# The attention softmax's maxima and sums: two row layouts swapped through DRAM instead of by matmuls on tables

## The chip, the cores and the metric

The kernel runs on one core of a Trainium2 chip. The metric is device time in microseconds (us). The core's engines run side by side and wait for each other through semaphores: TensorE (PE; its weight loads are listed apart as PEld), VectorE (DVE), ScalarE (ACT), GpSimd (POOL) and SyncE (SP). SP and POOL issue the DMAs that matter here; all of them share sixteen DMA engines.

## The reference

One layer of a decoder trunk on a sequence of 512 tokens with 1024 features: a feed-forward half step, a mixer of an attention branch and an mLSTM branch, and a second feed-forward half step. The change touches the attention branch alone: four head slots, and in each slot three groups with (window, dilation) = (128, 1), (512, 4), (2048, 16). The outputs of a slot's groups are added with weights that come from each group's maximum m and sum l:

```python
    m = jnp.max(s, axis=-1)
    p = jnp.exp(s - m[..., None])
    l = jnp.sum(p, axis=-1)
    ...
    lse = jnp.moveaxis(m + jnp.log(l), -1, 2)
    ...
    alpha = jax.nn.softmax(jnp.stack(lses, axis=0), axis=0)
    att = jnp.sum(alpha[..., None] * jnp.stack(outs, axis=0), axis=0)
```

So for each token the maxima and sums of the groups must meet.

## The kernel before

The projections are float32 products, each split into three passes of a reduced-precision matmul: every weight tile of 128x1024 is loaded by SP (`wf`, three buffers), cast on ACT to a high half (`wh`) and subtracted on DVE to a low half (`wl`, both with five buffers, line 99), and PE multiplies high by high, high by low and low by high (`ws`, line 189: 24 matmuls of 512 columns for each of two tiles of a group).

The attention part handles one head slot h after another. `scores(h)` computes the score blocks in PSUM, and DVE adds the mask and takes each row's maximum. The tile `val` holds, for 128 partitions, the maxima in `val[:, 0, :]` and the sums in `val[:, 1, :]`. Its columns 0 to 3 belong to the first group, whose rows lie in blocks of 128 tokens in a row (token = 128*b + p: the "natural" layout). Its columns 4 to 7 belong to the two dilated groups, masked and reduced together, whose rows lie by residue class (token = 4*p + j: the "class" layout). ACT then computes the exponentials (line 929), whose row sums are the second half of `val`.

`exchange(h)` brings both layouts together. DVE multiplies the values with 0/1 tables (`perm`, loaded once by POOL) into two spread tiles, `ln` and `lc` (lines 937 and 939, 128x128 each, for maxima and for sums). PE then multiplies these with two more tables into a PSUM bank `pe` (lines 943 and 945; a float32 matmul of the program counts as two in the trace). From `pe` DVE reads the other layout's maxima `om` and sums `ol`: `mm` (joint maximum), `ee` (two differences, exponentiated on ACT, line 954), `l` (two products), `w` (sum, reciprocal, product), and last the scaling of the eight score blocks `sm` by `w` (line 964). `turn(h)` transposes the scaled blocks on PE into the banks `pt` (line 973) and ACT copies them to `pT`; `values(h)` multiplies them with the attention values.

Program order puts other work between these: for h = 1, 2, 3 the loop runs `qk_proj(h, 0)`, `exchange(h - 1)`, `qk_proj(h, 1)`, `turn(h - 1)`, `qk_proj(h, 2)`, `values(h - 1)` and `scores(h)`. The last slot's `exchange(3)` stands between two projections of the mLSTM branch (tile `pm`, followed on DVE by a convolution whose steps write `z`), and `turn(3)` stands in the middle of the second of them. A list scheduler merges the code into one instruction order for each engine; each engine then runs its list strictly in order.

POOL's list is short in this part: constants, then for each pair of slots a store of the projected values to a DRAM scratch tensor (`v12rows`, line 897) and a load of it in class layout (`v`, line 899).

Of the kernel before, what the change touches and what calls it, by code (L numbers as in the profile page):

```python
# [10 lines left out]
F32 = mybir.dt.float32  # L11
# [3 lines left out]
ALU = mybir.AluOpType  # L15

P = 128
T = 512
# [21 lines left out]
def tile_hybrid_block(ctx: ExitStack, tc: tile.TileContext, a: dict):  # L40
    nc = tc.nc
# [20 lines left out]
    def bank(name):  # L62
        return psum.tile([P, 512], F32, tag="pp", name=name)

    def pair(name):
        return [bank(f"{name}_{b}") for b in range(2)]
# [65 lines left out]
    dram = ctx.enter_context(tc.tile_pool(name="dram", bufs=1, space=bass.MemoryType.DRAM))  # L132
# [667 lines left out]
    ap_ = actx.enter_context(tc.tile_pool(name="attn", bufs=1))  # L800
# [5 lines left out]
    masks = ap_.tile([P, 512], BF16, name="masks")  # L806
    with tc.issue_after(mixer_from):
        nc.gpsimd.dma_start(masks, a["masks"])
    perm = ap_.tile([P, 72], F32, name="perm")
    nc.gpsimd.dma_start(perm, a["perm"])  # L810
    by4, by32, mod4, div32 = perm[:, 0:32], perm[:, 32:64], perm[:, 64:68], perm[:, 68:72]
    gb = mix.tile([4, 2], F32, name="gb")
    with tc.issue_after(mixer_from):
        nc.gpsimd.dma_start(gb, a["gbias"])
# [89 lines left out]
    def scores(h):  # L904
        q = [qk_of[h, g] for g in range(3)]
        ps0, ps1 = pair(f"ps0{h}"), pair(f"ps1{h}")
        for tb in range(NT):
            lo = 0 if tb else P
            nc.tensor.matmul(ps0[tb // 2][:, tb % 2 * 256 + lo:(tb % 2 + 1) * 256], lhsT=q[0][:, 0, tb * P:(tb + 1) * P],
                             rhs=q[0][:, 1, max(tb - 1, 0) * P:(tb + 1) * P], start=True, stop=True)  # L910
        for g in (1, 2):
            for j in range(NT):
                o = j % 2 * 256 + (g - 1) * P
                nc.tensor.matmul(ps1[j // 2][:, o:o + P], lhsT=q[g][:, 0, j * P:(j + 1) * P], rhs=q[g][:, 1, j * P:(j + 1) * P], start=True, stop=True)
        sm = ap_.tile([P, 8, 256], F32, tag="sm", bufs=1, name=f"sm{h}")
        val = small.tile([P, 2, 8], F32, tag="val", name=f"val{h}")
        nm = small.tile([P, 8], F32, tag="nm", name=f"nm{h}")
        for half, ps in enumerate((ps0, ps1)):
            for i in range(NT):
                lo = P if half == 0 and i == 0 else 0  # L920
                nc.vector.tensor_tensor_reduce(out=sm[:, 4 * half + i, lo:], in0=ps[i // 2][:, i % 2 * 256 + lo:(i % 2 + 1) * 256],
                                               in1=masks[:, half * 256 + lo:(half + 1) * 256], scale=1.0, scalar=NEG,
                                               op0=ALU.add, op1=ALU.max,
                                               accum_out=val[:, 0, 4 * half + i:4 * half + i + 1])
            hs = slice(4 * half, 4 * half + 4)
            nc.vector.tensor_scalar(nm[:, hs], val[:, 0, hs], -SC, None, op0=ALU.mult)
        for i in range(8):
            lo = P if i == 0 else 0
            nc.scalar.activation(sm[:, i, lo:], sm[:, i, lo:], AF.Exp, scale=SC, bias=nm[:, i:i + 1],
                                 accum_out=val[:, 1, i:i + 1])  # L930
        return sm, val

    def exchange(h, sm, val):
        ln = ap_.tile([P, 8, 32], F32, tag="ln", bufs=1, name=f"ln{h}")
        lc = ap_.tile([P, 2, 32, 4], F32, tag="lc", bufs=1, name=f"lc{h}")
        for v in range(2):
            nc.vector.tensor_tensor(ln[:, 4 * v:4 * v + 4, :], val[:, v, 0:4, None].broadcast_to([P, 4, 32]),
                                    by4[:, None, :].broadcast_to([P, 4, 32]), op=ALU.mult)
            nc.vector.tensor_tensor(lc[:, v, :, :], by32[:, :, None].broadcast_to([P, 32, 4]),
                                    val[:, v, None, 4:8].broadcast_to([P, 32, 4]), op=ALU.mult)  # L940
        pe = bank(f"pe{h}")
        for v in range(2):
            nc.tensor.matmul(pe[:, 8 * v:8 * v + 4], lhsT=lc[:, v].rearrange("p a b -> p (a b)"), rhs=div32,
                             start=True, stop=True)
            nc.tensor.matmul(pe[:, 8 * v + 4:8 * v + 8],
                             lhsT=ln[:, 4 * v:4 * v + 4].rearrange("p a b -> p (a b)"), rhs=mod4,
                             start=True, stop=True)
        om, ol = pe[:, 0:8], pe[:, 8:16]
        mm_ = small.tile([P, 8], F32, tag="mm", name=f"mm{h}")
        nc.vector.tensor_tensor(mm_, val[:, 0, :], om, op=ALU.max)  # L950
        ee = small.tile([P, 2, 8], F32, tag="ee", name=f"ee{h}")
        nc.vector.tensor_tensor(ee[:, 0, :], val[:, 0, :], mm_, op=ALU.subtract)
        nc.vector.tensor_tensor(ee[:, 1, :], om, mm_, op=ALU.subtract)
        nc.scalar.activation(ee, ee, AF.Exp, scale=SC)
        l = small.tile([P, 2, 8], F32, tag="l", name=f"l{h}")
        nc.vector.tensor_tensor(l[:, 0, :], ee[:, 0, :], val[:, 1, :], op=ALU.mult)
        nc.vector.tensor_tensor(l[:, 1, :], ee[:, 1, :], ol, op=ALU.mult)
        w = small.tile([P, 8], F32, tag="w", name=f"w{h}")
        nc.vector.tensor_tensor(w, l[:, 0, :], l[:, 1, :], op=ALU.add)
        nc.vector.reciprocal(w, w)  # L960
        nc.vector.tensor_tensor(w, w, ee[:, 0, :], op=ALU.mult)
        for i in range(8):
            lo = P if i == 0 else 0
            nc.vector.tensor_scalar(sm[:, i, lo:], sm[:, i, lo:], w[:, i:i + 1], None, op0=ALU.mult)
# [158 lines left out]
    with tc.issue_after(v0_done[-1].ins):  # L1123
        parts57()
    sm, val = scores(0)


# [39 lines left out]
    caus = mix.tile([P, 1, P], F32, name="caus")  # L1167
    with tc.issue_after(mixer_from):
        nc.gpsimd.dma_start(caus[:, 0, :], a["caus"])
    for h in range(1, HEADS):  # L1170
        qk_proj(h, 0)
        exchange(h - 1, sm, val)
        qk_proj(h, 1)
        pT = turn(h - 1, sm)
        if h == 3:
            gates_turn()
        qk_proj(h, 2)
        values(h - 1, pT, v12)
        if h == 2:
            gates()  # L1180
            hg = work.tile([P, 1, D], F32, tag="gain", bufs=2, name="hg")
            nc.gpsimd.dma_start(hg[:, 0, :], a["mlstm_head_g"].partition_broadcast(P))
            v12 = v12_proj(1)
        sm, val = scores(h)
    pqs = [m_qk_proj(0, 0)]
    exchange(3, sm, val)
    tail = []
    pqs.append(m_qk_proj(0, 1, lambda: tail.append(turn(3, sm))))
# [241 lines left out]
def _consts():  # L1430
    half = 16
    inv = np.power(np.float32(500000.0), -(np.arange(half, dtype=np.float32) * np.float32(2.0) / np.float32(32.0)))
    ang = np.arange(T, dtype=np.float32)[None, :] * inv.astype(np.float32)[:, None]
    c, s = np.cos(ang).astype(np.float32), np.sin(ang).astype(np.float32)
    import ml_dtypes

    def rope(u, v):
        r = np.concatenate([u, v])
        return np.concatenate([r, r.reshape(32, P, 4).transpose(0, 2, 1).reshape(32, T)])[:, None, :]

    p = np.arange(P)[:, None]
    i = np.arange(P)[None, :]
    masks = np.zeros((P, 512), np.float32)
    masks[:, 0:128] = np.where(p - (i - P) <= 128, 0.0, NEG)
    masks[:, 128:256] = np.where(p - i >= 0, 0.0, NEG)
    masks[:, 256:384] = masks[:, 128:256]
    masks[:, 384:512] = np.where((p - i >= 0) & ((p - i) % 4 == 0), 0.0, NEG)
    perm = np.zeros((P, 72), np.float32)
    c32, c4 = np.arange(32)[None, :], np.arange(4)[None, :]
    perm[:, 0:32] = p // 4 == c32  # L1450
    perm[:, 32:64] = p % 32 == c32
    perm[:, 64:68] = p % 4 == c4
    perm[:, 68:72] = p // 32 == c4
    sel = np.zeros((4, MH * P), np.float32)
    for h in range(MH):
        sel[h, h * P:(h + 1) * P] = 1.0
    caus = np.where(np.arange(P)[None, :] >= p, 0.0, -NEG).astype(np.float32)
    return {
        "ropeC": rope(c, c), "ropeS": rope(-s, s),
        "masks": masks.astype(ml_dtypes.bfloat16), "sel": sel, "caus": caus, "perm": perm,  # L1460
    }


# [70 lines left out]
```

## Time and profile before

| | |
|---|---|
| device time, 3 runs | 1332.76, 1333.11, 1333.22 us; median 1333.11 us |
| profiled execution, first to last instruction | 1330.7 us |
| median less span (what lies around it) | 2.4 us |
| PE, PEld, DVE, ACT, POOL busy | 1322.2, 1195.5, 1005.4, 642.1, 79.7 us |
| granted TensorE clock, mean | 0.999 |
| bytes moved by DMA | 156.33 MB, mean 117 GB/s |

The span counts from the first to the last instruction of one profiled execution; the device time of a run holds some start and end around it. The four head slots' exchanges start on PE at 442.2, 484.1, 548.7 and 591.4 us after the span's start.

### The profile page before, as it was taken

What the parts mean: (1) busy time and instruction counts of PE and PEld (TensorE: products, weight loads), DVE (VectorE), ACT (ScalarE), POOL (GpSimd) and SP (SyncE); (2) the same over time, 40 slices, a digit from 0 to 9 for tenths busy, and PEclk for the clock granted to TensorE, in tenths of its full rate; (3) what the DMA queues carried; (4) which work ended last, traced back from release to release, by engine and by line L of the source; (5) the groups of instructions that cost most, each with busy time, mean ns of one, the idle gap of its engine ahead of it and who ended that gap; (6) DMA issues with size and microseconds to landing.
All of it is one profiled execution on the core that took longest, in us unless ns stands there. A gap on an engine that the chain in (4) does not pass through costs nothing.

```text
span 1330.7 us, 20773 instructions
## 1 busy us (share of the span) xinstructions
PE 1322.2 (99%) x8277; PEld 1195.5 (90%) x8277; DVE 1005.4 (76%) x1547; ACT 642.1 (48%) x1040; POOL 79.7 (6%) x118
## 2 busy tenths in 40 slices
PE   9999999999999999999999999999999999999997
PEld 8999999888998888888888889999889999999886
DVE  7999898798765556575756777776379899897887
ACT  6444444566634544544545444444265444445663
POOL 1000000330300000000000000000010000001220
PEclk9999999999999999999999999999999999999999
DMA  5333332896433422412222212325413333335981
GB/s 198 96 104 110 104 105 96 207 240 162 136 113 117 143 68 91 159 64 80 80 79 80 67 60 79 96 96 183 156 42 97 110 112 101 107 112 144 267 175 64
DMA packets 43746, 156.33 MB, mean 117 GB/s; under 512 B 4965, under 2 KB 4973, under 8 KB 43393
## 3 DMA queue, kind: packets, MB, share of 16 engines
q1 hardware_dynamic: 32832, 116.18, 26.4%
q0 software_dynamic: 10800, 38.82, 11.9%
q8 instruction: 65, 1.06, 0.3%
q14 instruction: 33, 0.26, 0.1%
q10 hardware_dynamic: 16, 0.00, 0.0%
HBM read 148.69 MB, written 6.29 MB: 116 GB/s over the span
## 4 chain that ended last, share of the span: by engine, by line
PE 98%; DVE 1%; DMA 0%; POOL 0%; ACT 0%; issue 0%; DVEq 0%; POOLq 0%; ACTq 0%
PE qb_b L338 10%; PE qb_a L338 10%; PE pq L189 8%; PE pm L189 7%; PE p L189 6%; PE qa_b L338 4%; PE qa_a L338 4%; PE qb_gm L1090 4%; PE acc_o L243 3%; PE accb_b L537 3%; PE accb_a L537 3%; PE pvo L1216 2%; PE pvo L1217 2%; PE pvo L1218 2%; PE accc_b L537 2%; PE accc_a L537 2%
## 5 line engine op out<-in xcount | busy, mean ns | idle before, releaser
L189 PE MATMUL pq<-hTh_mx,wh_qk 128*128 128x512 f32 x160 | 63.2, 395 | 0.0
L189 PE MATMUL pq<-hTl_mx,wh_qk 128*128 128x512 f32 x160 | 62.4, 390 | 0.0
L99 DVE TENSOR_TENSOR wl_qk<-wf_qk,wh_qk 128x1024 fp32r<-128x1024 f32 x24 | 29.4, 1224 | 30.9 <-ACT wh_qk L85 14.2
L189 PE MATMUL pm<-hTh_mx,wh_mqk 128*128 128x512 f32 x128 | 50.3, 393 | 0.0
L1216 PE MATMUL pvo<-wh_vo,hTh_mx 128*128 128x512 f32 x128 | 50.2, 392 | 0.0
L189 PE MATMUL pm<-hTl_mx,wh_mqk 128*128 128x512 f32 x128 | 49.9, 390 | 0.0
L1218 PE MATMUL pvo<-wl_vo,hTh_mx 128*128 128x512 f32 x128 | 49.9, 390 | 0.0
L1217 PE MATMUL pvo<-wh_vo,hTl_mx 128*128 128x512 f32 x128 | 49.8, 389 | 0.0
L99 DVE TENSOR_TENSOR wl_mqk<-wf_mqk,wh_mqk 128x1024 fp32r<-128x1024 f32 x16 | 19.6, 1225 | 35.7 <-ACT wh_mqk L85 26.7
L85 ACT CAST wh_qk<-wf_qk 128x1024 fp32r<-128x1024 f32 x24 | 25.0, 1046 | 40.6 <-issue 11.6
L263 ACT CAST wh_a<-cd_a 128x1024 fp32r<-128x1024 f32 x19 | 19.9, 1049 | 40.8 <-DVE cd_a L263 40.8
L189 PE MATMUL pq<-hTh_mx,wl_qk 128*128 128x512 f32 x160 | 39.6, 389 | 0.0
L263 ACT CAST wh_b<-cd_b 128x1024 fp32r<-128x1024 f32 x19 | 19.9, 1049 | 40.6 <-DVE cd_b L263 40.6
L338 PE MATMUL qa_a<-hTh_f,wh_a 128*128 128x256 f32 x152 | 38.2, 284 | 0.0
L338 PE MATMUL qa_b<-hTh_f,wh_b 128*128 128x256 f32 x152 | 38.2, 284 | 0.0
L338 PE MATMUL qa_a<-hTl_f,wh_a 128*128 128x256 f32 x152 | 38.1, 283 | 0.0
L338 PE MATMUL qa_b<-hTl_f,wh_b 128*128 128x256 f32 x152 | 38.1, 283 | 0.0
L85 ACT CAST wh_mqk<-wf_mqk 128x1024 fp32r<-128x1024 f32 x16 | 16.8, 1049 | 41.9 <-PE pvo L1217 22.9
L1011 DVE SCALAR_TENSOR_TENSOR z<-pm,cw,z 128x511 f32<-128x511 f32 (+2 forms) x48 | 35.3, 744 | 1.4 <-ACT z L1009 0.9
L189 PEld LDWEIGHTS pq<-hTh_mx,wl_qk 128*128 128x128 f32 x160 | 30.0, 188 | 6.2
L189 PEld LDWEIGHTS pq<-hTh_mx,wh_qk 128*128 128x128 f32 x160 | 30.1, 188 | 6.0
L189 PEld LDWEIGHTS pq<-hTl_mx,wh_qk 128*128 128x128 f32 x160 | 30.1, 188 | 6.0
(684 smaller groups left out, 4552.4 us busy)
## 6 DMA issues: line engine op xcount, KB each, us to landing
wf_qk<-in_wqk SPq DMA_DIRECT2D x24, 512.0 KB, 3.3
g_a<-in_wgu SPq DMA_DIRECT2D x19, 512.0 KB, 3.8
u_a<-in_wgu SPq DMA_DIRECT2D x19, 512.0 KB, 3.8
g_b<-in_wgu SPq DMA_DIRECT2D x19, 512.0 KB, 3.8
u_b<-in_wgu SPq DMA_DIRECT2D x19, 512.0 KB, 3.8
wf_mqk<-in_wmqk SPq DMA_DIRECT2D x16, 512.0 KB, 3.4
wf_vo<-in_wvo SPq DMA_DIRECT2D x16, 512.0 KB, 3.4
T_a<-in_wdq POOLq DMA_DIRECT2D x12, 512.0 KB, 10.2
```

Of the source, the lines that this page charges most:

```text
L85: return nc.scalar.copy(wh, wf)
L99: nc.vector.tensor_tensor(wl[:, :m], wf[:, :m], wh[:, :m].bitcast(F32), op=ALU.subtract)
L189: nc.tensor.matmul(out, lhsT=wt[:, k * P:(k + 1) * P], rhs=x[:, k, 0:T], start=n == 0, stop=n == len(terms) - 1)
L243: nc.tensor.matmul(out, lhsT=x[:, tk], rhs=w[:, cs], start=first and n == 0, stop=last and n == 2, skip_group_check=True)
L263: self.last[eng] = getattr(getattr(nc, eng), fn)(*args, **kw).ins
L338: nc.tensor.matmul(out, lhsT=wt[:, i * P:(i + 1) * P], rhs=y[:, i, :], start=first and n == 0, stop=last and n == len(terms) - 1, skip_gro ...
L537: nc.tensor.matmul(o, lhsT=x[:, tk], rhs=w[:, cs], start=k in "1256" and g + m + n == 0, stop=False, skip_group_check=True)
L1011: nc.vector.scalar_tensor_tensor(z[:, s:], src[:, :T - s], cw[:, ct, 3 - s:4 - s], z[:, s:], op0=ALU.mult, op1=ALU.add)
L1090: nc.tensor.matmul(out, lhsT=wt[:, i * P:(i + 1) * P], rhs=y[:, i, :], start=first and m == 0, stop=last and m == len(terms) - 1, skip_gro ...
L1216: nc.tensor.matmul(out, lhsT=hTh[:, k, tk], rhs=wh[:, cs], start=k == 0, stop=False)
L1217: nc.tensor.matmul(out, lhsT=hTl[:, k, tk], rhs=wh[:, cs], start=False, stop=False)
L1218: nc.tensor.matmul(out, lhsT=hTh[:, k, tk], rhs=wl[:, cs], start=False, stop=k == KD - 1)
```

## The change

The tables `perm` and the spread tiles `ln` and `lc` go, and with them in each head slot four DVE products and four matmuls. A new function `trade` is called twice in `scores`, once when the maxima are there and once when the sums are. It issues four DMAs on POOL's queue: the natural columns and the class columns are stored to two small DRAM tensors `nat` and `cla` of 512 floats, each in token order, and each is loaded back in the other layout into a new tile `others[h]` (named `other` in the trace and in the order). `exchange` reads `om` and `ol` from that tile.

```diff
@@ tile_hybrid_block
-    perm = ap_.tile([P, 72], F32, name="perm")
-    nc.gpsimd.dma_start(perm, a["perm"])
-    by4, by32, mod4, div32 = perm[:, 0:32], perm[:, 32:64], perm[:, 64:68], perm[:, 68:72]
@@ scores
             nc.vector.tensor_scalar(nm[:, hs], val[:, 0, hs], -SC, None, op0=ALU.mult)
+        trade(h, val, 0)
         for i in range(8):
             ...
+        trade(h, val, 1)
         return sm, val
 
+    others = {}
+
+    def trade(h, val, v):
+        nat, cla = (dram.tile([T], F32, name=f"{n}{h}{v}") for n in ("nat", "cla"))
+        blocks = lambda x: x.rearrange("(b p) -> p b", p=P)
+        classes = lambda x: x.rearrange("(p j) -> p j", j=4)
+        if v == 0:
+            others[h] = ap_.tile([P, 2, 8], F32, tag="other", bufs=2, name=f"other{h}")
+        nc.gpsimd.dma_start(blocks(nat), val[:, v, 0:4])
+        nc.gpsimd.dma_start(classes(cla), val[:, v, 4:8])
+        nc.gpsimd.dma_start(others[h][:, v, 4:8], classes(nat))
+        nc.gpsimd.dma_start(others[h][:, v, 0:4], blocks(cla))
+
     def exchange(h, sm, val):
-        ln = ap_.tile([P, 8, 32], F32, tag="ln", bufs=1, name=f"ln{h}")
-        lc = ap_.tile([P, 2, 32, 4], F32, tag="lc", bufs=1, name=f"lc{h}")
-        for v in range(2):
-            nc.vector.tensor_tensor(ln[:, 4 * v:4 * v + 4, :], val[:, v, 0:4, None].broadcast_to([P, 4, 32]),
-                                    by4[:, None, :].broadcast_to([P, 4, 32]), op=ALU.mult)
-            nc.vector.tensor_tensor(lc[:, v, :, :], by32[:, :, None].broadcast_to([P, 32, 4]),
-                                    val[:, v, None, 4:8].broadcast_to([P, 32, 4]), op=ALU.mult)
-        pe = bank(f"pe{h}")
-        for v in range(2):
-            nc.tensor.matmul(pe[:, 8 * v:8 * v + 4], lhsT=lc[:, v].rearrange("p a b -> p (a b)"), rhs=div32,
-                             start=True, stop=True)
-            nc.tensor.matmul(pe[:, 8 * v + 4:8 * v + 8],
-                             lhsT=ln[:, 4 * v:4 * v + 4].rearrange("p a b -> p (a b)"), rhs=mod4,
-                             start=True, stop=True)
-        om, ol = pe[:, 0:8], pe[:, 8:16]
+        om, ol = others[h][:, 0, :], others[h][:, 1, :]
```

The store of `nat` and the load in `blocks` form go in pieces of one float (512 pieces of 4 bytes); the store of `cla` and the load in `classes` form go in 128 pieces of four floats.

The new DMAs stand in POOL's list among the transfers of the attention values. From the `perm` load to the second load of `v`, POOL's list before reads (`hg` is a gain that the mLSTM branch uses later):

```order
L810 DMA perm<-in_perm 128x72
L897 DMA v12rows_4734<-v12flat_4729 128x4x512
L899 DMA v_0_4736<-v12rows_4734 128x2048
L1182 DMA hg<-in_mlstm_head_g 128x1024
L897 DMA v12rows_5570<-v12flat_5565 128x4x512
L899 DMA v_1_5572<-v12rows_5570 128x2048
```

In the changed kernel the same list reads for head slot 0, from the store of the values on (`nat_4779`, `cla_4780` carry the maxima, `nat_4794`, `cla_4795` the sums):

```order
L894 DMA v12rows_4732<-v12flat_4727 128x4x512
L940 DMA nat_4779<-val_4767 128x4x1
L941 DMA cla_4780<-val_4767 128x4
L896 DMA v_0_4734<-v12rows_4732 128x2048
L942 DMA other_4781<-nat_4779 128x4
L943 DMA other_4781<-cla_4780 128x4x1
L940 DMA nat_4794<-val_4767 128x4x1
L941 DMA cla_4795<-val_4767 128x4
L942 DMA other_4781<-nat_4794 128x4
L943 DMA other_4781<-cla_4795 128x4x1
```

The two stores of the maxima come ahead of the load of `v`, everything else of this slot's trade comes behind it. Slot 2 has the same shape around the second load of `v`, there with `nat` of the sums ahead of it and `cla` of the sums behind the loads of the maxima; slots 1 and 3 have eight small DMAs and nothing between them: `nat`, `cla`, `nat` of the sums, load, `cla` of the sums, and the other three loads.

On DVE the last slot's exchange changes places with the convolution. Before, from the last spread product to the scaling:

```order
L939 TENSOR_TENSOR lc_6011<-perm,val_5928 128x128
L99 TENSOR_TENSOR wl_vo_6234<-wf_vo_6230,wh_vo_6232 128x1024
L1011 SCALAR_TENSOR_TENSOR z_6155<-pm_0_5948,cw,z_6155 128x511
L1011 SCALAR_TENSOR_TENSOR z_6155<-pm_0_5948,cw,z_6155 128x510
L1011 SCALAR_TENSOR_TENSOR z_6155<-pm_0_5948,cw,z_6155 128x509
L99 TENSOR_TENSOR wl_vo_6264<-wf_vo_6260,wh_vo_6262 128x1024
L950 TENSOR_TENSOR mm_6021<-val_5928,pe_6016 128x8
L1011 SCALAR_TENSOR_TENSOR z_6155<-pm_1_5949,cw,z_6155 128x511
```

In the changed kernel, the same stretch up to the last product `l`:

```order
L99 TENSOR_TENSOR wl_vo_6240<-wf_vo_6236,wh_vo_6238 128x1024
L948 TENSOR_TENSOR mm_6027<-val_5932,other_5946 128x8
L1009 SCALAR_TENSOR_TENSOR z_6161<-pm_0_5965,cw,z_6161 128x511
L950 TENSOR_TENSOR ee_6029<-val_5932,mm_6027 128x8
L951 TENSOR_TENSOR ee_6029<-other_5946,mm_6027 128x8
L1009 SCALAR_TENSOR_TENSOR z_6161<-pm_0_5965,cw,z_6161 128x510
L954 TENSOR_TENSOR l_6033<-ee_6029,val_5932 128x8
L1009 SCALAR_TENSOR_TENSOR z_6161<-pm_0_5965,cw,z_6161 128x509
L955 TENSOR_TENSOR l_6033<-ee_6029,other_5946 128x8
```

Then come the three small steps of `w`, as before, and after them, where before the scaling is followed by a weight subtraction:

```order
L962 TENSOR_SCALAR sm_5931<-sm_5931,w_6036 128x128
L962 TENSOR_SCALAR sm_5931<-sm_5931,w_6036 128x256 x7
L1009 SCALAR_TENSOR_TENSOR z_6161<-pm_1_5966,cw,z_6161 128x511
L99 TENSOR_TENSOR wl_vo_6270<-wf_vo_6266,wh_vo_6268 128x1024
L1009 SCALAR_TENSOR_TENSOR z_6161<-pm_1_5966,cw,z_6161 128x510
L1009 SCALAR_TENSOR_TENSOR z_6161<-pm_1_5966,cw,z_6161 128x509
```

`mm`, which reads the returned maxima, has moved ahead of the first convolution half (`pm_0`), and the second half (`pm_1`) has moved behind the scaling. In slots 0 and 2 one weight subtraction of line 99 has moved from ahead of `mm` to between the two products `l`; in slot 1 one has moved behind the scaling. PE's list loses the four matmuls of each exchange and is otherwise the same; SP's list is the same.

More of the change, by code (lines that the diff above doesn't have):

```diff
@@ L1447, in _consts @@
     masks[:, 384:512] = np.where((p - i >= 0) & ((p - i) % 4 == 0), 0.0, NEG)
[L1448 to L1453, printed above, removed]
     sel = np.zeros((4, MH * P), np.float32)
@@ L1459, in _consts @@
         "ropeC": rope(c, c), "ropeS": rope(-s, s),
-        "masks": masks.astype(ml_dtypes.bfloat16), "sel": sel, "caus": caus, "perm": perm,
+        "masks": masks.astype(ml_dtypes.bfloat16), "sel": sel, "caus": caus,
     }
```

## Prediction

> **What bounds the kernel now.** I read the page first: the busy shares, and the shares of the chain of work that ended last.
>
> ```profile
> span 1330.7 us, 20773 instructions
> PE 1322.2 (99%) x8277; PEld 1195.5 (90%) x8277; DVE 1005.4 (76%) x1547; ACT 642.1 (48%) x1040; POOL 79.7 (6%) x118
> ...
> PE 98%; DVE 1%; DMA 0%; POOL 0%; ACT 0%; issue 0%; DVEq 0%; POOLq 0%; ACTq 0%
> ```
>
> TensorE (PE) is busy for 99% of the span and carries 98% of the chain. Then the view of waits, for PE alone; it has two rows in all:
>
> ```profile
> PE warm L74 <- DVE nhalf L81: 1.1, 1, 1.1
> PE g_f1pre L691 <- DVE gcol L263: 0.3, 1, 0.3
> ```
>
> PE waits 1.4 us in the whole program, all of it at the start. So a microsecond taken out of PE's list is a microsecond of time, as long as nothing that PE needs comes late; and work on DVE, ACT or POOL counts only once it makes PE wait.
>
> **What PE loses.** The timeline of PE around the first exchange: start, length, line and tiles of each group.
>
> ```profile
> 434.90 1.98 PE L189 MATMUL pq<-hTh_mx,wl_qk 128*128 128x512 f32 x8
> 436.71 0.39 PE L189 MATMUL pq<-hTh_mx,wh_qk 128*128 128x512 f32 x1
> ...
> 440.34 1.98 PE L189 MATMUL pq<-hTh_mx,wl_qk 128*128 128x512 f32 x8
> 442.16 0.28 PE L943 MATMUL pe<-perm,lc 128*128 128x4 f32 x2
> ...
> 442.97 0.48 PE L189 MATMUL pq<-hTh_mx,wh_qk 128*128 128x512 f32 x1
> 443.29 0.40 PE L189 MATMUL pq<-hTl_mx,wh_qk 128*128 128x512 f32 x1
> 443.52 0.39 PE L189 MATMUL pq<-hTh_mx,wh_qk 128*128 128x512 f32 x1
> ```
>
> Lengths overlap, since matmuls are pipelined; I count from start to start. Eight projections take 1.81 us where the next projection follows (434.90 to 436.71), so without the exchange the projection that starts at 442.97 would start at 440.34 + 1.81 = 442.15: 0.82 us. The first projection behind the exchange also holds the next one back for 0.32 us (442.97 to 443.29), where the usual step is 0.23 (443.29 to 443.52): another 0.09. One exchange costs PE 0.91 us. The last of the four shows the same 0.81 between its first matmul and the next projection:
>
> ```profile
> 591.44 0.28 PE L943 MATMUL pe<-perm,lc 128*128 128x4 f32 x2
> ...
> 592.25 0.48 PE L189 MATMUL pm<-hTh_mx,wh_mqk 128*128 128x512 f32 x1
> ```
>
> Four exchanges: 4 x 0.9 = 3.6 us gone from PE. More can't come from it, since PE has no waits here that could vanish as well.
>
> **What DVE loses** is worth nothing by itself: the sixteen spread products, by these two groups 16 x 0.29 = 4.7 us, ran under PE's projections, and so did the load of the tables.
>
> ```profile
> L937 DVE TENSOR_TENSOR ln<-val,perm x8: 283/292/294, 432.6 to 582.3; 128x128 f32<-128x128 f32 x8
> L939 DVE TENSOR_TENSOR lc<-perm,val x8: 286/292/295, 432.9 to 584.3; 128x128 f32<-128x128 f32 x8
> ```
>
> **What comes instead: 32 small DMAs on POOL's queue.** Their issue first. In the timeline of POOL the second figure is the issue's own length, the bracket its idle time before:
>
> ```profile
> 429.78 0.78 POOL L897 DMA_DIRECT2D v12rows<-v12flat  x1 [69.84 <-ACT v12flat L895]
> 436.14 0.54 POOL L899 DMA_DIRECT2D v<-v12rows  x1 [5.58 <-DMA v12rows<-v12flat]
> 523.28 0.54 POOL L1182 DMA_DIRECT2D hg<-in_mlstm_head_g  x1 [86.61 <-DVE Gl L1155]
> ...
> 543.61 0.53 POOL L899 DMA_DIRECT2D v<-v12rows  x1 [6.54 <-PE pq L189]
> ```
>
> A store in 512 pieces takes 0.78 us to issue, a load in 128 rows 0.54. I price the 16 one-float transfers by the first and the 16 four-float ones by the second: 16 x 0.78 + 16 x 0.54 = 21 us over 150 us, in which POOL was idle. The loads of `v` stay where they are, since the two or three stores put ahead of them are issued while POOL waits for `v12rows`.
>
> The unknown is L, the time of one such DMA from issue to landing. Before has no transfer in 4- or 16-byte pieces. The nearest rows of the list of DMA issues (the last figure is the median to landing, in us):
>
> ```profile
> v12rows<-v12flat POOLq DMA_DIRECT2D x2, 1024.0 KB, 6.4
> v<-v12rows POOLq DMA_DIRECT2D x2, 1024.0 KB, 5.2
> ...
> cw<-in_convwb POOLq DMA_DIRECT2D x1, 40.0 KB, 3.2
> ...
> selr<-in_sel POOLq DMA_DIRECT2D x1, 8.0 KB, 2.1
> ```
>
> The lower end is 2.1 (four rows), the upper 6.4 (512 pieces stored to the same DRAM scratch, but 1 MB of them). Nearest in bytes and in number of pieces is `cw`, 128 rows of 320 bytes, at 3.2; 512 pieces take 0.24 longer to issue (0.78 against 0.54). I take L = 3.4 for all of them.
>
> **Do they land in time?** What PE needs is the scaled blocks `sm` for `turn`, so I compare s, the start of the scaling, with T, the start of PE's transposes. The steps from the returned sums to the scaling, and the scaling itself:
>
> ```profile
> 444.36 0.16 DVE L957 TENSOR_TENSOR l<-ee,pe 128x8 f32<-128x8 f32 x1
> ...
> 445.19 2.13 DVE L964 TENSOR_SCALAR sm<-sm,w 128x128 f32<-128x128 f32 x8
> ```
>
> So s is 0.83 behind the landing of the last load, and the scaling takes 2.13. The transposes of slots 0 to 3, with the projection that follows the first:
>
> ```profile
> 453.96 1.80 PE L973 MATMUL pt<-ident,sm 128*128 128x128 f32 x15
> 455.51 0.47 PE L189 MATMUL pq<-hTh_mx,wh_qk 128*128 128x512 f32 x1
> ...
> 495.91 1.80 PE L973 MATMUL pt<-ident,sm 128*128 128x128 f32 x15
> ...
> 560.52 0.71 PE L973 MATMUL pt<-ident,sm 128*128 128x128 f32 x5
> ...
> 597.80 1.80 PE L973 MATMUL pt<-ident,sm 128*128 128x128 f32 x15
> ```
>
> Fifteen transposes take 1.55 us (to 455.51) and the scaling 2.13, block by block, so s must be some 1.0 ahead of T (an estimate: the difference and 0.4 for the last block). T itself comes 0.9 earlier, by the matmuls that go. Deadlines for s, on the clock of before: 452.1, 494.0, 558.6 and 595.9.
>
> Slots 0 and 2: the trade queues behind the 1 MB load of `v`, which lands 5.2 after its issue, at 441.3 and 548.8. Behind that a store and a load must land, in slot 0 with one more issue between: s = 441.3 + 0.54 + 2L + 0.83 = 442.7 + 2L, and s = 548.8 + 2L + 0.83 = 549.6 + 2L. Slots 1 and 3: POOL's strict order makes three landings follow each other (store of the maxima, its load's issue, store `cla` of the sums, last load), counted from the last maximum:
>
> ```profile
> 474.45 0.08 DVE L921 DVE_READ_ACCUMULATOR2_ANT val<- 128x1 f32 x1
> ...
> 581.78 0.08 DVE L921 DVE_READ_ACCUMULATOR2_ANT val<- 128x1 f32 x1
> ```
>
> s = 474.53 + 0.54 + 3L + 0.83 = 475.9 + 3L, and 583.2 + 3L. In slot 3 something else is due as well: three convolution steps and a weight subtraction have moved behind the scaling, and ACT's tanh and its copies to `pT` follow them, ahead of the value products:
>
> ```profile
> 594.52 0.74 DVE L1011 SCALAR_TENSOR_TENSOR z<-pm,cw,z 128x509 f32<-128x509 f32 x1
> ...
> 597.18 1.06 ACT L1013 ACTIVATE th<-z 128x1024 f32<-128x1024 f32 x1
> 598.32 2.00 ACT L976 COPY pT<-pt 128x384 f32<-128x384 f32 x4
> ...
> 604.93 1.73 PE L984 MATMUL o<-pT,v 128*128 128x128 f32 x14
> ```
>
> 2.13 + 3 x 0.74 + 1.22 + 1.06 + 2.00 = 8.6 before 604.93 - 0.9 = 604.0: s by 595.4, a little sooner than 595.9.
>
> With L = 3.4 the four s are 449.5, 486.1, 556.4 and 593.4, ahead of their deadlines by 2.6, 7.9, 2.2 and 2.0 us. Nothing is late. The thresholds are L = 4.0 (slot 3), 4.5 (slot 2), 4.7 (slot 0) and 6.0 (slot 1). Past them PE waits 3, 2, 2 and 3 us for each microsecond of L.
>
> The waits of `mm` and of the second `l` block DVE for a few microseconds, and the weight subtractions behind them (line 99) come later. Their cover is the five buffers: the next such row already waits for PE to give a buffer back, and by the order its weights are read four weight tiles later, over 20 us at 5.45 us a tile (434.90 to 440.34).
>
> ```profile
> 442.42 1.22 DVE L99 TENSOR_TENSOR wl_qk<-wf_qk,wh_qk 128x1024 fp32r<-128x1024 f32 x1 [2.24 <-PE pq L189]
> ```
>
> If that cover were gone, PE would next wait for `wl`. ACT's small exponential of `ee` now stands ahead of a copy of a projection bank; that bank comes round again only eight banks later.
>
> **Sum.** -3.6 on PE, 0 for everything else: a span of 1330.7 - 3.6 = 1327.1 us. The median of the runs is 2.4 above that span, so 1333.1 - 3.6 = 1329.5 us. A measurement of this kernel can tell about 0.2% (2.7 us) from no change.
>
> **Rivals.**
> Slow landings, a part of the gain: L between 4.3 and 5.2. At L = 4.85 the waits are 3 x 0.85 in slot 3 and 0.7 and 0.4 in slots 2 and 0, together 3.6: 1333.1, no change. For it speaks that each trade moves 512 single floats to scratch DRAM and back, a kind of transfer that no row shows; against it that `cw`, in 128 pieces with twenty times the bytes (40 KB against 2), lands in 3.2.
> Slow landings that cost more than they save, from L = 5.25 on. At the upper end, 6.4, PE waits 7.1, 3.8, 3.5 and 1.1 us in slots 3, 2, 0 and 1, 15.5 in all: 1345. Only a transfer of 1 MB took that long here.
> The Trainium skill's page "DMA: Bandwidth & Descriptors" says in its section "Rules for kernel authors" that a last dimension that isn't contiguous becomes one descriptor for each element, and in "Specifications" that a transfer of less than 512 bytes is a read-modify-write. It speaks for these two rivals but prices neither; the same page's fixed cost of about 2.0 us for a DMA (section "Anatomy of one DMA") would give L near 2, an estimate by that page, and no wait.
> POOL held up by DVE: each issue waits for the DVE instruction that runs, at most the 1.22 of a weight subtraction. Three hops in slot 3 put s at 593.4 + 3.7 = 597.1, 1.7 late, two in slot 2 at 558.8, 0.2 late: 1333.1 - 3.6 + 1.9 = 1331.4. Against it: the issue at 429.78 ran inside such a subtraction and still took only 0.78.
>
> ```profile
> 429.37 1.22 DVE L99 TENSOR_TENSOR wl_qk<-wf_qk,wh_qk 128x1024 fp32r<-128x1024 f32 x1
> ```
>
> The Trainium skill's page "SBUF — State Buffer" describes this as a trap (section "SBUF: two separate sides"): while DVE runs a two-port operation, GpSimd can't write its descriptors. By this trace it doesn't occur beside the subtractions of line 99.
> The freed time doesn't come back, because PE then waits for weights: 1333.1. Against it stands PE's 1.4 us of waits in all.
>
> **Chances.** All hidden 0.70; a part of the gain 0.10; slower 0.13; POOL held up 0.04; time not given back 0.03. Faster by over 0.2% needs the waits below 0.9 us (L up to 4.3): 0.70. Within 0.2%: 0.10 + 0.04 + 0.03 = 0.17. Slower: 0.13. The predicted time is 1329.5. The range goes from 1328.9 (each exchange worth a tenth more, and 0.2 for the spread of the runs) to 1333.0, which takes in the partial cases up to L = 4.85 and leaves the slower one out; it holds some 0.82.
>
> **What would show it.** In the profile after: no matmuls of `pe`, and projections that follow each other in steps of 0.23 there; small DMAs that land in 2 to 4 us; rows of `mm` and of the second `l` on DVE that wait for DMA; and no new row for PE in the view of waits. It is wrong if transposes of `sm` or value products wait for DVE or ACT; the landings of `nat` and of the loads in single floats would tell why.

## The result, and the profile after

| | median of the runs, us | from, to | ratio to before, 95% interval |
|---|---|---|---|
| before, on the same chip | 1332.93 | 1332.75, 1333.22 | |
| changed kernel | 1371.06 | 1370.26, 1372.66 | 1.0289 [1.0276, 1.0301] |

The change made the kernel 38 us slower, where 3.6 us faster was forecast. The page of the changed kernel, the busy shares and the shares of the chain:

```profile
span 1368.5 us, 20742 instructions
PE 1327.4 (97%) x8245; PEld 1198.9 (88%) x8245; DVE 1002.0 (73%) x1531; ACT 641.0 (47%) x1040; POOL 100.1 (7%) x149
...
PE 81%; issue 8%; DMA 7%; DVE 1%; POOL 1%; ACT 1%; POOLq 0%; DVEq 0%; SPq 0%; ACTq 0%
```

PE ran 32 matmul instructions less and was busy for 5 us more. In the view of waits, PE alone has one new row; the row of DVE below it is from the view for all engines, and the columns are total, times and longest:

```profile
PE pt L971 <- DVE sm L962: 32.6, 4, 10.8
PE warm L74 <- DVE nhalf L81: 1.1, 1, 1.1
PE g_f1pre L691 <- DVE gcol L263: 0.3, 1, 0.3
...
DVE mm L948 <- DMA other<-cla: 62.2, 4, 19.7
```

PE's transposes waited in each of the four slots, for the scaled blocks `sm`. Behind that DVE stood at `mm` for the values that come back by DMA. The view of DMA issues says which DMAs came late (last figure: median to landing):

```profile
nat<-val POOLq DMA_DIRECT2D x8, 2.0 KB, 11.1
cla<-val POOLq DMA_DIRECT2D x8, 2.0 KB, 9.9
other<-nat POOLq DMA_DIRECT2D x8, 2.0 KB, 6.1
other<-cla POOLq DMA_DIRECT2D x8, 2.0 KB, 3.1
...
v<-v12rows POOLq DMA_DIRECT2D x2, 1024.0 KB, 11.8
```

The stores of 512 single floats took 11.1 us and not 3.4. The loads in single floats, `other<-cla`, took 3.1. `cla` goes in 128 pieces of 16 bytes, stands behind a `nat` in the queue, and was nearly as late (9.9); `v`, behind it too, went from 5.2 to 11.8. The timeline of POOL in slot 1 (start, length, and in the bracket the idle time before and what ended it) shows that the stores came free one after another:

```profile
482.04 0.77 POOL L940 DMA_DIRECT2D nat<-val  x1 [24.33 <-DVE nm L923]
483.67 0.56 POOL L941 DMA_DIRECT2D cla<-val  x1 [0.87 <-DVE nm L923]
484.24 0.75 POOL L940 DMA_DIRECT2D nat<-val  x1
492.82 0.56 POOL L942 DMA_DIRECT2D other<-nat  x1 [7.83 <-DMA nat<-val]
493.37 0.55 POOL L941 DMA_DIRECT2D cla<-val  x1
493.92 0.76 POOL L943 DMA_DIRECT2D other<-cla  x1
501.44 0.54 POOL L942 DMA_DIRECT2D other<-nat  x1 [6.77 <-DMA nat<-val]
```

The first `nat` releases its load 10.8 us after its issue, the second, issued 2.2 us later, another 8.6 us behind the first. Last, PE's clock, in the table of windows (window, length, busy time of PE, PEld, DVE, ACT and POOL, granted clock, DMA share, GB/s): the stretch behind the wait of each slot.

```profile
461.00:464.70 3.70, 3.70 (x16) 3.56 (x17) 3.70 (x9) 1.80 (x4) 0.00 (x0) 0.50 0.00 0
509.40:513.00 3.60, 3.60 (x17) 3.47 (x18) 3.60 (x9) 3.54 (x7) 0.00 (x0) 0.55 0.00 0
583.77:590.00 6.23, 6.23 (x32) 5.43 (x33) 6.23 (x13) 3.81 (x7) 0.00 (x0) 0.68 0.46 139
633.00:639.00 6.00, 6.00 (x22) 5.40 (x23) 5.96 (x12) 0.98 (x2) 0.00 (x0) 0.50 0.23 70
```

After each wait PE came back at half clock (in slots 1 and 2 the window reaches past the end of it, so its mean is higher). What is missing there, length times (1 - clock), is 1.9 + 1.6 + 2.0 + 3.0 = 8.5 us. So the loss adds up: 32.6 of waits, 8.5 of low clock, less about 4 that PE gained (measured below), make 37 of the 37.8 by which the span grew.

### The profile page after: what moved, and what is told of

It is laid out like the page before. It is cut to its first block, busy times and chain, and to the rows that moved or that the text cites. A ratio compares the mean times of both kernels' runs of the same rounds, so it can differ in the third digit from the quotient of the medians.

```text
span 1368.5 us, 20742 instructions
## 1 busy us (share of the span) xinstructions
PE 1327.4 (97%) x8245; PEld 1198.9 (88%) x8245; DVE 1002.0 (73%) x1531; ACT 641.0 (47%) x1040; POOL 100.1 (7%) x149
## 4 chain that ended last, share of the span: by engine, by line
PE 81%; issue 8%; DMA 7%; DVE 1%; POOL 1%; ACT 1%; POOLq 0%; DVEq 0%; SPq 0%; ACTq 0%
PE qb_b L338 10%; PE qb_a L338 10%; PE p L189 6%; PE pm L189 5%; PE qa_a L338 4%; PE qa_b L338 4%; DMA nat<-val 4%; PE qb_gm L1088 4%; PE acc_o L243 3%; PE accb_b L537 3%; PE accb_a L537 3%; PE pvo L1214 2%; PE pvo L1216 2%; PE pvo L1215 2%; DMA cla<-val 2%
## 5 line engine op out<-in xcount | busy, mean ns | idle before, releaser
L971 PE MATMUL pt<-ident,sm 128*128 128x128 f32 x60 | 13.9, 425 | 32.6 <-DVE sm L962 32.6
L85 ACT CAST wh_qk<-wf_qk 128x1024 fp32r<-128x1024 f32 x24 | 25.0, 1046 | 37.9 <-PE pq L189 11.1
L971 PEld LDWEIGHTS pt<-ident,sm 128*128 128x128 f32 x60 | 12.1, 223 | 34.5 <-DVE sm L962 23.0
```

Of the source, the lines that this page charges most:

```text
L971: nc.tensor.transpose(pt[:, i * P:(i + 1) * P], sm[:, 4 * half + 2 * b + i // 2, (i % 2) * P:(i % 2 + 1) * P], ident)
```

## The experiments

Three questions stood. Is PE's gain there at all, once nothing waits? Why are these DMAs slow: because any small DMA is (B), because each single float has its price wherever it goes (A1), or because of where the single floats go, side by side in DRAM (A2)? And is the wait the whole loss, or do the stores also hold up the weights, and the clock PE?

**No exchange at all.** Both calls of `trade` go, and `exchange` joins each block's maxima and sums with themselves, so the layouts are not swapped and the weights of the groups are other numbers.

```diff
-        trade(h, val, 0)
-        trade(h, val, 1)
-        om, ol = others[h][:, 0, :], others[h][:, 1, :]
+        om, ol = val[:, 0, :], val[:, 1, :]
```

> The exchange's matmuls and spread products are left out, and no DMA takes their place: the joint maximum and sum are formed from the block's own values, so the layouts are not swapped. If the gain on PE was sized right, 1333.0 - 3.6 = 1329.4 us and no wait of PE behind the scaling of sm. If the 3.6 us were only moved (PE then waits for weights), about 1333.

Measured: 1328.46 us (1328.35 to 1328.89), ratio 0.9968 [0.9957, 0.998], span 1326.5, and PE waits only in its two old rows. What PE can gain is 4.3 us, and this is the floor for any exchange that PE doesn't do.

**`nat` in pieces of 16 bytes.** The natural columns are stored as each partition has them, 128 pieces of four floats, and read back by four loads in single floats.

```diff
-        nc.gpsimd.dma_start(blocks(nat), val[:, v, 0:4])
+        nc.gpsimd.dma_start(classes(nat), val[:, v, 0:4])
-        nc.gpsimd.dma_start(others[h][:, v, 4:8], classes(nat))
+        for b in range(4):
+            nc.gpsimd.dma_start(others[h][32 * b:32 * b + 32, v, 4:8],
+                                nat.rearrange("(r j b) -> b r j", j=4, b=4)[b])
```

> nat is stored in 128 pieces of 16 bytes instead of 512 of 4, and read back in the other layout by four loads of 128 single floats each; no store in single floats is left. Theory A (a store in single floats drains slowly, some 8 to 9 us for 512 pieces, and holds what is queued behind it): landing of nat and cla falls from some 10 to 4 us, PE waits under 5 us in all, 1330 to 1337 us. Theory B (any small DMA through DRAM takes some 10 us, whatever its pieces): landings stay at 10 us and the time at about 1370 us, or above for the six DMAs more in each slot.

Measured: 1329.02 us (1328.93 to 1329.53), ratio 0.9972 [0.9961, 0.9983]. Its DMA issues:

```profile
other<-nat POOLq DMA_DIRECT2D x32, 0.5 KB, 3.7
nat<-val POOLq DMA_DIRECT2D x8, 2.0 KB, 3.1
cla<-val POOLq DMA_DIRECT2D x8, 2.0 KB, 2.4
other<-cla POOLq DMA_DIRECT2D x8, 2.0 KB, 3.1
```

With 24 DMAs more on POOL the loss is gone. So B is out: small DMAs on POOL's queue land in 2.4 to 3.7 us. The slow ones were the stores in single floats.

**The single floats apart.** The store still has 512 pieces of 4 bytes, but the tokens lie 256 bytes apart in DRAM.

```diff
-        nat, cla = (dram.tile([T], F32, name=f"{n}{h}{v}") for n in ("nat", "cla"))
+        wide = dram.tile([T, 64], F32, name=f"nat{h}{v}")
+        nat = wide[:, 0]
+        cla = dram.tile([T], F32, name=f"cla{h}{v}")
```

> As the changed kernel, but the tokens of nat lie 256 bytes apart in DRAM, so no two stored floats share a line of 64 bytes; the load of nat then goes in single floats as well. Theory A1 (each small piece has its price, wherever it lies): nat lands 10 us after its issue as before, 1370 us. Theory A2 (the pieces hold each other up because they share a line): nat lands in 3 to 4 us, and the time falls to 1330 to 1345 us.

Measured: 1328.43 us in one run, span 1326.5, no new wait of PE; `nat` landed in 4.0 us, `cla` in 3.0, the loads in 3.1 and 3.0. The same number of pieces, of the same size, from the same partitions, was no longer slow. That rules out A1 and leaves A2: it is the neighbourhood of the pieces in DRAM. The line of 64 bytes that the expectation names is a guess, and is put to the test below.

**The DMAs without a use.** The kernel before, its matmuls in place, with the 32 DMAs of the change added; nobody reads what they bring.

```diff
+        trade(h, val, 0)
         ...
+        trade(h, val, 1)
```

> The kernel before, with its exchange by matmuls, and beside it all 32 DMAs of the change, whose loaded values nobody reads. If the loss is the wait for the values alone: landings of 10 us as in the changed kernel, no wait of PE, 1333 us. If the DMAs also hold up the weights so far that PE waits for them: PE waits at projections, 1335 us or more.

Measured: 1333.15 us (1332.9 to 1334.65), ratio 1.0006 [0.9997, 1.0015], with `nat` at 10.3 and `cla` at 9.1 us: as slow as in the changed kernel, and free. One wait came with them:

```profile
PE ps L914 <- DVE qk L838: 1.0, 1, 1.0
```

By the median the unused DMAs cost 0.4 us. The runs fall into two groups, though: six took 1332.9 to 1333.3, and four, the profiled one among them, 1334.3 to 1334.7. So nearly the whole loss of the changed kernel comes from what waits for the values; what the stores take from other work costs at most some 1.6 us here.

**PE kept busy while it waits.** The changed kernel, with products of the identity ahead of each `turn`, for about as long as PE waited there.

```diff
+    FILL = (34, 23, 40, 48)
+    def hold(h):
+        hb = bank(f"hold{h}")
+        with tc.issue_after(last_mm[0]):
+            for i in range(FILL[h]):
+                nc.tensor.matmul(hb[:, 0:P], lhsT=ident, rhs=ident, start=True, stop=True)
     def turn(h, sm):
+        hold(h)
```

> The changed kernel, with extra products of the identity with itself (34, 23, 40 and 48 of them in slots 0 to 3, into a PSUM bank that nobody reads) put behind the last projection ahead of each `turn`, so that PE works while it would wait for `sm`. Theory that the granted clock of about 0.50 after each wait is a part of the loss: the clock stays at 1.0 through the transposes, the fifteen transposes take 1.8 us again in place of 3.5, and the time falls by the 8 to 9 us that the half clock costs, to 1362 or 1363. Rival that the waits are the whole loss and the clock is an accident of the record: no change, 1371. By both the wait for the values itself stays, now as time of the extra products.

Measured: 1364.06 us (1362.24 to 1365.5), ratio 1.0238 [1.0221, 1.0256] against 1.0289 [1.0276, 1.0301]. The added products of slot 0 and the transposes behind them, in the timeline of PE:

```profile
452.98 7.75 PE L971 MATMUL hold<-ident 128*128 128x128 f32 x68
460.57 2.24 PE L981 MATMUL pt<-ident,sm 128*128 128x128 f32 x15
```

And the window around them (columns as above):

```profile
450.00:465.00 15.00, 15.00 (x108) 13.58 (x107) 7.25 (x21) 7.48 (x13) 1.30 (x2) 1.00 0.17 46
```

With work that nobody needs, as long as the wait was, the clock stayed at 1.00, and the span fell by 8.2 us (1368.5 to 1360.3), the times by 7.0. The half clock was a real part of the loss. The times fell a little less than the 8 to 9 that was expected. A part of the difference is that the fillers outlast the waits: PE no longer waits for `sm` at all, and in slot 2 its transposes start 1.2 us after the scaling does (579.14 to 580.37), where in slot 1 0.3 us lie between them (506.92 to 507.26).

**How far apart.** The 256 bytes of the earlier edit became 16 and 64 (`[T, 4]` and `[T, 16]` for `[T, 64]`).

> The changed kernel with the single floats of `nat` 16 bytes apart in DRAM (four tokens in 64 bytes) in place of 4. If stores into the same 64 bytes hold each other up, `nat` still lands late (about 10 us) and the time is near 1370. If only stores that lie within 16 bytes of each other do, `nat` lands in about 4 us and the time is near 1329.

> The changed kernel with the single floats of `nat` 64 bytes apart in DRAM, one to each 64 bytes. If what the stores share is 64 bytes or less, `nat` lands in about 4 us, as it did at 256 bytes, and the time is near 1329. If it is a longer piece, `nat` lands late (6 to 10 us) and the time is well above 1330.

Measured: 1329.33 us at 16 bytes and 1328.77 at 64, one run each; `nat` landed in 4.9 and 4.3 us. At 16 bytes a short wait of PE is left:

```profile
PE pt L973 <- DVE sm L964: 0.6, 1, 0.6
```

With 4 bytes at 11.1 and 256 at 4.0 the landing falls step by step. Four stores in each 64 bytes hardly hurt, sixteen in each do.

**Another queue.** Both stores issued by SP, whose queue brings the weights.

```diff
-        nc.gpsimd.dma_start(blocks(nat), val[:, v, 0:4])
-        nc.gpsimd.dma_start(classes(cla), val[:, v, 4:8])
+        nc.sync.dma_start(blocks(nat), val[:, v, 0:4])
+        nc.sync.dma_start(classes(cla), val[:, v, 4:8])
```

> The changed kernel with the stores of `nat` and `cla` issued by SP, whose queue else brings the weights, and the loads left on POOL. If the stores are slow because of where their pieces go in DRAM, they land about 10 us after issue here too, the weights behind them come late as well, and the time is 1370 or more. If POOL's queue is what is slow with 512 pieces, they land in about 3 us and the time is near 1330.

Measured: 1367.12 us, one run; PE waited 30.1 us for `sm`.

```profile
nat<-val SPq DMA_DIRECT2D x8, 2.0 KB, 13.6
cla<-val SPq DMA_DIRECT2D x8, 2.0 KB, 12.3
```

The stores are slow on either queue: POOL's queue isn't the cause. The time was expected at 1370 or more and is 3 us below that.

**The store by itself.** In a later stretch of over 200 us in which POOL is idle (behind the attention part, in the kernel with `nat` 256 bytes apart), stores that nobody uses, each with a load behind it that waits for it:

```diff
+            r = dram.tile([4, P * gap], F32, name=f"t{n}_{key}")
+            piece = r.rearrange("b (p g) -> p b g", g=gap)[0:parts, 0:cols, 0]
+            with tc.issue_after(last):
+                nc.gpsimd.dma_start(piece, nhalf[0:parts, 0:cols])
+                last = nc.gpsimd.dma_start(got[0:1, 4 * n:4 * n + 1], piece[0:1, 0:1]).ins
```

> The kernel with `nat` 256 bytes apart, and behind its last attention work, in a stretch of over 200 us in which POOL is idle, twelve stores that nobody uses, each followed by a load of one float of what it stored, so that one is landed before the next starts. Six store 512 floats at 4, 8, 16, 32, 64 and 256 bytes from partition to partition; then one column alone (128 floats side by side, and again 256 bytes apart), and four columns of 32, 16 and 8 partitions (four runs of 128, 64 and 32 bytes); the store in steps of 4 bytes stands twice. A quiet store takes about 3 us, the one at 4 bytes 8 to 10. If stores into the same 64 bytes go one after another (some 0.5 us each, 16 of them), one column, 32 and 16 partitions are as slow as all 512, 8 partitions half as slow, and 8 bytes apart about 6. If it is 512 bytes (128 stores, 0.06 us each), one column is as slow, 32 partitions land in about 4.5 and 16 in about 3.5. If the whole store has one price for each piece that is not alone, one column and 32 partitions both land in about 4.5.

Each geometry came once (the 4-byte step twice), and the result was mixed: 10.8, 6.3, 2.6, 2.2, 2.2 and 3.6 us for steps of 4, 8, 16, 32, 64 and 256 bytes, but one column took 6.6 side by side and also 6.1 at 256 bytes, where no two pieces are close. Of the four columns, 32 partitions took 5.3, 16 took 4.6 and 8 took 1.7. Some stores had met weight loads and some not. So the stores were repeated in other orders.

> The stores of the probe again (without the 32-byte step), each geometry two or three times and in shuffled order, since in the first run some of them met weight loads and some did not (one column 256 bytes apart, which should be quiet, took 6.1 us). If the geometry sets the time, 4 bytes apart stays at 9 to 11 us each time, 8 bytes apart near 6, 16, 64 and 256 bytes at 2 to 4, and the column 256 bytes apart falls to 2 to 4 where no weight load is under way. If what the store happens to meet sets it, the times of one geometry differ as much as those between geometries. Among the partial stores (one column, 32, 16 and 8 partitions, all 4 bytes apart): equal and near 9 if a shared 64 bytes is filled one store at a time and nothing else counts; falling with the number of pieces (128, 128, 64, 32) if the DMA engines drain all of a store's pieces at one rate.

The DMA issues of this second run, medians of three (two for the 4-byte step):

```profile
t_by_eight<-nhalf POOLq DMA_DIRECT2D x3, 2.0 KB, 5.5
t_by_sixteen<-nhalf POOLq DMA_DIRECT2D x3, 2.0 KB, 4.0
t_by_sixtyfour<-nhalf POOLq DMA_DIRECT2D x3, 2.0 KB, 4.3
t_by_wide<-nhalf POOLq DMA_DIRECT2D x3, 2.0 KB, 4.0
t_onecol<-nhalf POOLq DMA_DIRECT2D x3, 0.5 KB, 8.3
t_rows_thirtytwo<-nhalf POOLq DMA_DIRECT2D x3, 0.5 KB, 4.7
t_rows_sixteen<-nhalf POOLq DMA_DIRECT2D x3, 0.2 KB, 1.7
t_rows_eight<-nhalf POOLq DMA_DIRECT2D x3, 0.1 KB, 3.0
t_onecol_wide<-nhalf POOLq DMA_DIRECT2D x3, 0.5 KB, 3.2
t_by_four<-nhalf POOLq DMA_DIRECT2D x2, 2.0 KB, 8.9
```

One column side by side, 128 floats in 512 bytes, is as slow as all four columns (8.3 and 8.9), and 128 floats 256 bytes apart land in 3.2: the number of pieces in the store doesn't set the time by itself. 128 floats in four runs of 128 bytes take 4.7, 64 floats in four runs of 64 bytes 1.7 (4.6 in the first run). So a shared 64 bytes isn't enough; that expectation failed. What seems to count is how many of the pieces go into the same stretch of some hundred bytes. An estimate from these rows, 2 us and 0.05 for each piece into the same 512 bytes, gives 8.4 for 128 of them, 5.2 for 64 and 3.6 for 32, near the slow rows (8.3 and 8.9; 5.5; 4.0 and 4.7). The quick rows it doesn't order: it gives 2.8 for 16 pieces, 2.4 for 8 and 2.1 for 2, where 1.7, 3.0 to 4.3 and 3.2 to 4.0 were measured. A stretch of 256 bytes would fit hardly worse; the runs don't decide the size, nor why such pieces hold each other up. From issue to the release of their loads, stores of one geometry differ by 0.6 to 4.9 us from time to time (`by_wide` 2.5, 4.2 and 7.4). The weight loads that they meet are the likely reason: the two stores that met almost no other traffic (1 GB/s), one at 64 and one at 256 bytes, both took 2.5.

These unused stores weren't free. The two kernels with the probe took 1337.97 and 1335.66 us, one run each, 9.7 and 7.4 more than the same kernel without it (1328.24, in the next experiment). In the first of them PE has two new waits in that stretch, 1.9 us at 1025.4 and 4.0 at 1065.4. The chain that ended last leads each back to a weight load of the second feed-forward half step that was issued 1 to 2 us after a store in steps of 4 bytes. For the second wait it reads:

```profile
1049.01 12.94 DMA u_b<-in_wgu
```

The other load took 12.5 us; the median of these loads is 3.7. So here the stores do hold up the weights for so long that PE waits.

**The version that beats both.** The kernel with `nat` 256 bytes apart, timed closely:

> The kernel with the tokens of `nat` 256 bytes apart once more, timed against the kernel before. Theory: the exchange through DRAM, with landings of 3 to 4 us, hides wholly and gives back what the matmuls took, so 1328.5 (4.2 below before, 0.3%), level with the kernel without any exchange (1328.46). Rival that a part of the waits is left: 1329.5 or more.

Measured: 1328.24 us (1328.08 to 1328.78), ratio 0.9967 [0.9955, 0.9979]: 4.4 us or 0.3% faster than before, level with the kernel without any exchange (1328.46). PE has no wait for `sm` in it. The exchange through DRAM is wholly hidden there.

## Why the prediction was wrong

**The step that failed is "I take L = 3.4 for all of them", and the bracket 2.1 to 6.4 around it.** I took a transfer's price from rows that agreed in bytes and in the number of pieces, and held a store of 1 MB (6.4) for an upper end that 2 KB couldn't pass. Both rows move pieces of hundreds of bytes or more. `nat` writes 4 bytes 128 times into each 512, and that is where the price is: the same 512 pieces cost 11.1 us side by side and 4.0 apart. One L for all was wrong as well: the last loads took 3.1, near the 3.4, and the stores three times that. The single floats were in the diff, and the prediction named them as a reason for two rivals; that they lie side by side in DRAM it never asked.

**The path was right.** DVE waits for the returned values, the scaling comes late, and PE's transposes wait for it: that is the chain that the prediction drew. Rows of PE's timeline, with the wait in the bracket:

```profile
461.00 3.51 PE L971 MATMUL pt<-ident,sm 128*128 128x128 f32 x15 [7.62 <-DVE sm L962]
...
509.40 3.45 PE L971 MATMUL pt<-ident,sm 128*128 128x128 f32 x15 [5.29 <-DVE sm L962]
...
583.77 3.51 PE L971 MATMUL pt<-ident,sm 128*128 128x128 f32 x15 [8.88 <-DVE sm L962]
...
633.00 3.43 PE L971 MATMUL pt<-ident,sm 128*128 128x128 f32 x15 [10.78 <-DVE sm L962]
```

Put into the prediction's deadlines and formulas, these four waits give L = 8.5, 7.8, 9.0 and 7.7. That they agree so well is partly luck, for no landing of the four chains took just this long: slow and quick ones are mixed in it. The view of the chain that ended last has, for slot 3, the three landings that the prediction put behind each other (start, length):

```profile
605.59 10.97 DMA nat<-val
618.43 10.37 DMA cla<-val
629.08 2.55 DMA other<-cla
```

Slot 1 has the same three, with 10.5, 11.1 and 3.1. In slots 0 and 2 the prediction counted a store and a load behind the landing of `v`. There `v` took 11.8 in place of the 5.2 that it was given; in slot 0 the store took 11.7, some of it behind `v`; and in slot 2 POOL waited for the first `nat`, which took 17.8 and landed after `v`, with 6.1 and 2.5 for the store and the load behind it. Where the stores land in 3 to 4 us, the waits are gone, and at 4.9 a wait of 0.6 is left, as the thresholds of 4.0 to 6.0 said.

**What the waits cost besides was no term of the sum.** A microsecond of PE's wait was priced at a microsecond. Here 32.6 us of waits brought another 7 to 8.5 of half clock. With these waits put in, the prediction's sum would have come to 1333.1 - 3.6 + 32.6 = 1362, and still missed 9. Before has no wait of this length on PE, so no row showed it. The Trainium skill's page "TensorE: Matmul & The Clock Gate" says it (section "Part 1: The HAM clock gate"): after an idle window of about 3.4 us the clock falls to half, until PE has been busy for about as long. The trace agrees, 0.50 after waits of 5.3 to 10.8 us, for three to four microseconds in slots 0 to 2; in slot 3 it lasted nearly 6.

**A DMA was priced as if it were alone.** `v`'s load was put at its old 5.2 behind the stores; it took 11.8. A weight load on SP's own queue, `wf_w`, issued at 489.14, took 14.9, where the one in the same stretch takes 3.3 in the kernel with `nat` apart. A window of slot 0 in the changed kernel shows it, behind the length and the engines' columns by clock, DMA share and GB/s:

```profile
437.00:443.00 6.00, 6.00 (x28) 4.97 (x27) 1.23 (x1) 3.15 (x6) 0.15 (x1) 1.00 1.15 44
```

The same window in the kernel with `nat` apart:

```profile
437.00:443.00 6.00, 6.00 (x28) 4.95 (x28) 1.23 (x1) 2.84 (x4) 2.69 (x4) 1.00 0.93 246
```

The DMA engines count as busy in both (where the times of packets overlap, the share passes 1), and move 44 GB/s in the one and 246 in the other. But they don't count as busy all the time: in slot 1, from 486 to 490, both stores of `nat` are under way and the share is 0.00. What the stores wait for in that time, no view shows. In the attention part the delays did little harm by themselves, since the unused DMAs cost 0.4 us there by the median; that the three buffers of `wf` hide them is likely but not shown. In the later stretch of the probe the unused stores cost 7 to 10.

**What held.** PE's term: the last `o` matmul starts 3.7 us earlier in the kernel with `nat` apart (608.2 to 604.5), the last `acc_o` 3.6 (989.0 to 985.4), against 3.6 forecast. The span gained 4.2 to 4.4 (two runs of that kernel); the other 0.6 to 0.8 lies behind 989, where nothing was changed, and stays open. No run takes DVE's products or POOL's issues out alone, but with no wait left the gain is PE's term, so they were worth nothing, as forecast. POOL was not held up by DVE: the issues of the exchange took 0.54 to 0.77 us. The freed time did come back.

**The rivals.** "Slow landings that cost more than they save", at 0.13, is what happened, with 7.7 to 9.0 in place of its 6.4 at most. It had the direction and the path, and 1345 for the time; no rival had the price of the stores or the half clock. The Trainium skill's rule that was set beside it ("DMA: Bandwidth & Descriptors", section "Specifications": a transfer under 512 bytes is a read-modify-write) points the same way as the probe, in which pieces that go into the same few hundred bytes seem to be written one after another. That 4 bytes at a stride of 256 are fast, though under 512 as well, the rule alone doesn't tell; no run shows the read-modify-write itself.

## What to carry to other kernels

Price a small DMA by where its pieces go in DRAM, not by bytes and count: here a store of single floats side by side was slow. Giving each float 16 bytes or more to itself made it cheap, and so did storing in the order of the partitions and sorting in the load (loads of single floats took 3 us). When no row shows such a transfer, the time of a much larger one is no upper bound. Ask what the work costs once it is late, and add the clock that PE loses after a wait of several microseconds. A slow transfer that nobody waits for may cost little, as the unused stores in the attention part did (0.4 us), or much, as those of the probe did (7 to 10). So look first at who waits, and then at what else shares the DMA engines.

## What the runs showed of the hardware

A store of 2 KB in 4-byte pieces side by side took 11.1 us to landing; the second of two in a row released its load 8.6 us after the first. What stood behind such stores came late: a 1 MB load on the same queue took 11.8 us in place of 5.2, with 44 GB/s moved in 6 us of it where 246 were moved with the pieces apart. Loads of 512 KB on the other queue took 14.9 in place of 3.3 in the attention part, and 12.5 to 13.5 in place of 3.7 where they were issued 1 to 4 us after such a store of the probe. At 256 bytes apart the store took 4.0, and in 16-byte pieces 3.1. In a single column 128 such pieces, 512 bytes in all, took nearly as long as all four columns (8.3 and 8.9). Loads of 2 KB in 4-byte pieces took 3.0 to 3.3 in the kernels with `nat` 64 and 256 bytes apart. After waits of 5.3 to 10.8 us PE ran 3 to 6 us at 0.50 of its clock.
